# Raw weight rows of the second and third pair of w_up rows trade buffers, and the last write moves to another queue

## The chip, the cores and the metric

The kernel runs on one NeuronCore of a Trainium2 chip. What counts is the device time of one execution in microseconds (us), as the median of several runs. Beside it one execution was profiled: every engine's instructions and every transfer with its times. The engines are named as in the profile: PE (TensorE, with PEld for its weight loads), DVE (VectorE), ACT (ScalarE), POOL (GpSimd) and SP (SyncE, which here only issues transfers). An engine works through its own instructions in program order and waits on semaphores of others.

## The reference, cut to what matters

A decoder block for 1024 tokens of width 1024: a norm, two parallel branches (sparse attention and a state-space layer), a merge, and then an MLP and a final norm. The change touches only the MLP and the final norm:

```python
    x = x + merged @ w_out[l]
    h2 = rmsnorm(x, norm_mlp_g[l])
    x = x + jnp.square(jax.nn.relu(h2 @ w_up[l])) @ w_down[l]
return rmsnorm(x, norm_final_g)
```

`w_up` is 1024 x 4096 and `w_down` 4096 x 1024.

## The kernel before, in words

Every product is made of fp32 operands split in a high and a low part, with three matmuls each (high x high, low x high, high x low). A low part is raw minus high, so each weight tile costs a cast on ACT (the high part) and a subtraction on POOL or DVE (the low part) before PE can use it. The functions `cast` (L1091) and `weights` (L108) do that; a tile named `w` is such a pair.

The product with `w_up` is done as a two-by-two block scheme with seven products instead of eight. A *pair* q (0 to 15) is one step of it: two raw tiles of `w_up` (128 x 1024 fp32, 512 KB each), number 2q and 2q + 1. In the text, `raw0` is the first, and `a21` and `a22` are the halves of the second. From them come four weight tiles:

- `wo`, the cast of `raw0` as it was loaded (`open_high`/`open_low` for pairs 0 and 1, `prep_open` for the others);
- `wa`, the cast of the sum tile `sa`, which `prep_s` makes with two DVE operations (L1115, L1116); `prep_a` casts it, and then turns `raw0` into other sums in place with two more DVE operations (L1122, L1123);
- `wb`, the cast of that changed `raw0` (`prep_b`), and `wc`, the cast of `a22` (`prep_c`).

The PE side of a pair is `p1` and `p2` (with `wo`), `p6` and `p5` (with `wa`), `p7` and `p3` (with `wb`) and `p4` (with `wc`), 12 matmuls each. `p7`, `p6` and `p4` go on adding in one PSUM tile `pa` of the pair: `p4` may not touch it until the DVE addition of `p7` (L1161) has read it. `sums` then forms four tiles on DVE (L1182 to L1185) and writes the activations to DRAM.

The order is written out by hand: what stands earlier in the code stands earlier on its engine. Pair 0 is woven into the end of the norm, `norm_split` transposing normed rows on PE (L977), ACT casting them (L981) and DVE making their low parts (L986). Pairs 1 and 2 get their `wo`, `p1` and `p2` there too, early. `t3_chunk` and `t4_rows` build two more operands, T3 and T4, by the same three steps (T4 with two further DVE operations, L1058 and L1059). A loop over q from 1 to 15 follows, in which `up_raw(q + 2)` loads two pairs ahead, then the product with `w_down` (lines from L1401 on PE), which reads the activations back from DRAM, and last the final norm (`final_a`, `final_b`).

Raw tiles lie in one of two places: two buffers `raw` of the pool `wpool`, or one tile `raw2` (two raws in one) of `mpool`. Before, even pairs use the former and odd ones the latter. Pair 1 is the exception: its first raw is loaded early in a `raw` buffer (`r[1]`) and opened there, and later both raws are loaded again as `raw2`. Pair 2's first raw (`r2`, L1307) takes the buffer that `r[1]` leaves, and so its load waits for `open_low(1)` (L1109). The second (`r2b`, L1335) takes the buffer that pair 0's `raw0` leaves after `prep_b(0)`.

`ep` is a pool whose tag e4 has five buffers, for the normed rows `xs`, for the results `e1` and `e2` and for the gains.

Of the kernel before, what the change touches and what calls it, by code (L numbers as in the profile page):

```python
# [19 lines left out]
P = 128  # L20
S = 1024
# [44 lines left out]
def hybrid_block(ctx: ExitStack, tc: tile.TileContext, a: dict, out: bass.AP, dbg=None):  # L66
    nc = tc.nc
# [35 lines left out]
    def load(pool, src, n):  # L103
        raw = pool.tile([P, n], F32, name="raw", tag="raw", bufs=nbuf[0])
        nc.sync.dma_start(raw, src)
        return raw
# [64 lines left out]
    wpool = ctx.enter_context(tc.tile_pool(name="wpool", bufs=1))  # L171
# [3 lines left out]
    with ExitStack() as st1:  # L175
        pss = {}
        for c in PO1:
            nm, n = {"d": ("dps", DP1), "s": ("sps", SP1), "x": ("xps", XP1)}[c]
# [464 lines left out]
    with ExitStack() as st2:  # L643
        pss = {}
        for c in PO2:
            nm, n = {"s": ("ssp", SB), "t": ("tps", CB), "o": ("ops", OB)}[c]
# [23 lines left out]
        def prep(g, b):  # L670
            qT = ap_.tile([P, 6, P], F32R, name="qT", tag="qT", bufs=2)
            nc.sync.dma_start(f32(qT), q_d[g][b])

            for n in range(b + 1):
                if (g, n) in vT:
                    continue
                hf, o = n // 4, (n % 4) * P
                for j in range(2):
                    if (g, j, hf) not in kT:
                        kT[g, j, hf] = kp.tile([P, 2, 512], F32R, name="kT", tag="kT", bufs=6)  # L680
                    nc.sync.dma_start(f32(kT[g, j, hf][:, :, o:o + P]), k_d[g][n][:, j])
                vT[g, n] = kp.tile([P, 2, 2, 64], F32R, name="vt", tag="vt", bufs=9)
                nc.sync.dma_start(f32(vT[g, n]), v_d[g][n])
            return qT, gates[:, g, b]
# [148 lines left out]
        first, second = [], []  # L833
# [39 lines left out]
    with ExitStack() as st3:  # L873
# [6 lines left out]
        def e4(name, shape=(P, S)):  # L880
            return ep.tile(list(shape), F32, name=name, tag="e4")

        def s4(name, shape):
            return ep.tile(list(shape), F32, name=name, tag="s4", bufs=S4B)
# [76 lines left out]
        c1, c2 = slice(0, 512), slice(512, 1024)  # L961
# [26 lines left out]
        def split_to(name, b, pt):  # L988
            low(*high(name, b, pt))
# [33 lines left out]
        def norm_d3(b):  # L1023
            V.tensor_tensor(xr[b][:, c1], xs[b][:, c2], xs[b][:, c1], op=ALU.subtract)
# [66 lines left out]
        def cast(x, n):  # L1091

            w = wpool.tile([P, 2, S], F32R, name="w", tag="w", bufs=nbuf[1])
            A.copy(w[:, 0, :n], x)  # L1094
            G.tensor_tensor(w[:, 1, :n], x, f32(w[:, 0, :n]), op=ALU.subtract)  # L1095
            return w

        def prep_open(q, raw0):
            u = us[q] = Pair()
            u.wo = cast(raw0, S)  # L1100
# [10 lines left out]
        def prep_s(q):  # L1111

            u = us[q]
            u.sa = s4("sa", (P, S))
            V.tensor_tensor(u.sa[:, c2], u.a21, u.a22, op=ALU.add)  # L1115
            V.tensor_tensor(u.sa[:, c1], u.sa[:, c2], u.raw0[:, c1], op=ALU.subtract)  # L1116

        def prep_a(q):
            u = us[q]
            u.wa = cast(u.sa, S)  # L1120

            V.tensor_tensor(u.raw0[:, c1], u.raw0[:, c1], u.a21, op=ALU.subtract)  # L1122
            V.tensor_tensor(u.raw0[:, c2], u.raw0[:, c2], u.sa[:, c1], op=ALU.subtract)  # L1123

        def prep_b(q):
            us[q].wb = cast(us[q].raw0, S)
# [4 lines left out]
        def p1(q):  # L1131
            u = us[q]
            u.pa, u.e1 = acc("pa"), e4("e1", (P, 2, 512))
            prod(u.pa, u.wo[:, :, c1], "B11", True)
            A.copy(u.e1[:, 0], u.pa)

        def p2(q):
            u = us[q]
            pb = acc("pb")
            prod(pb, u.wo[:, :, c2], "B21", True)  # L1140
            V.tensor_tensor(u.e1[:, 0], u.e1[:, 0], pb, op=ALU.add)

        def p2_square(q):
            square(us[q].e1[:, 0])

        def p6(q):
            u = us[q]
            u.e2 = e4("e2", (P, 2, 512))
            prod(u.pa, u.wa[:, :, c1], "T2", False)
            A.copy(u.e2[:, 0], u.pa)  # L1150

        def p5(q):
            u = us[q]
            u.pc = acc("pc")
            prod(u.pc, u.wa[:, :, c2], "T1", True)
            A.copy(u.e2[:, 1], u.pc)

        def p7(q):
            u = us[q]
            prod(u.pa, u.wb[:, :, c1], "T3", False)  # L1160
            V.tensor_tensor(u.e2[:, 1], u.e2[:, 1], u.pa, op=ALU.add)  # L1161
            square(u.e2[:, 1])

        def p3(q):
            u = us[q]
            prod(u.pc, u.wb[:, :, c2], "B22", False)
            V.tensor_tensor(u.e2[:, 0], u.e2[:, 0], u.pc, op=ALU.add)
# [24 lines left out]

        def up_raw(q):

            if q % 2:
                t = mpool.tile([P, 2, S], F32, name="raw2", tag="m")
                for i in range(2):
                    nc.sync.dma_start(t[:, i], a["w_up"][2 * q + i])
                raws[q] = t[:, 0], t[:, 1]
            else:  # L1200
                raws[q] = [load(wpool, a["w_up"][2 * q + i], S) for i in range(2)]

        def set_raws(q, raw0, a21, a22):
            us[q].raw0, us[q].a21, us[q].a22 = raw0, a21, a22

        def half_raws(q):
            r0, r1 = raws[q]
            set_raws(q, r0, r1[:, c1], r1[:, c2])
# [8 lines left out]
        def load_acts(k):  # L1217
            if k < 56:
                raw = wpool.tile([P, 2, 512], F32, name="raw", tag="raw", bufs=nbuf[0])
                nc.sync.dma_start(raw, act_d[k % 8][:, LEFT[k // 8]])  # L1220
                araw.append(raw)

        def fetch(u):

            n, q = divmod(u, 16)
            if n == 0:
                if q % 2 == 0:
                    xy.append(oppool.tile([P, 2, 2, 512], F32, name="xy", tag="opT"))
                dst, i, j = xy[q // 2][:, q % 2, 0], 0, 0
            elif n == 1:  # L1230
                dst, i, j = xy[q // 2][:, q % 2, 1], 0, 1
            elif n in (2, 5):
                if q % 4 == 0:
                    z.append(mpool.tile([P, 4, 512], F32, name="z", tag="m"))
                dst, i, j = z[-1][:, q % 4], 1, int(n == 2)
            else:
                return
            nc.scalar.dma_start(dst, a["w_down"][2 * q + i][:, j * 512:j * 512 + 512])  # L1238
# [53 lines left out]
        r = [load(wpool, a["w_up"][2 * q], S) for q in range(2)]  # L1292
# [11 lines left out]
                norm_d3(b - 1)  # L1304
            norm_b(b, (lambda: open_low(1)) if b == 7 else None)
        norm_d3(7)
        r2 = load(wpool, a["w_up"][4], S)  # L1307
        p1(0)
        for f in norm_split(6):
            low(*f)  # L1310
# [21 lines left out]
        t4 = [t4_rows(4), t4_rows(5)]  # L1332
        split_to("T4", 4, t4[0])
        split_to("T4", 5, t4[1])
        r2b = load(wpool, a["w_up"][5], S)  # L1335
        p5(0)
        t4 += [t4_rows(6), t4_rows(7)]
        split_to("T4", 6, t4[2])
        split_to("T4", 7, t4[3])
        up_raw(1)  # L1340
        half_raws(1)
        p7(0)
        prep_s(1)
        prep_a(1)
        p3(0)
        prep_b(1)
        p3_square(0)
# [3 lines left out]
        for q in range(1, 16):  # L1351
            n = q + 1
            if q + 2 < 16 and q > 0:
                up_raw(q + 2)
            if q == 15:
                for k in range(2):
                    load_acts(k)
            if q >= 3:
                p1(q)
                p2(q)  # L1360
            if n < 16 and n > 2:
                prep_open(n, raws[n][0])
                half_raws(n)
            if n == 2:
                set_raws(2, r2, r2b[:, c1], r2b[:, c2])
            if q >= 3:
                p2_square(q)
            if n < 16:
                prep_s(n)
            p6(q)  # L1370
            p5(q)
            if n < 16:
                prep_a(n)
            else:
                for u in range(AHEAD):
                    fetch(u)
            p7(q)
            if n == 16:
                prep(0)
            p3(q)  # L1380
            if n < 16:
                prep_b(n)
            p3_square(q)
            if n == 16:
                prep(1)
            p4(q)
            if n < 16:
                prep_c(n)
            else:
                prep(2)  # L1390
            sums(q)


        y = []
# [30 lines left out]
            rstds[b] = ep.tile([P, 1], F32, name="rstd", tag="rstd")  # L1425
            G.tensor_tensor(rstds[b], sq[:, 0:1], neghalf, op=ALU.pow)

        def final_b(b):
            V.scalar_tensor_tensor(y[b][:, c1], y[b][:, c1], rstds[b], gfin[:, c1], op0=ALU.mult, op1=ALU.mult)  # L1429
            nc.sync.dma_start(out[b * P:(b + 1) * P, c1], y[b][:, c1])  # L1430
            A.activation(y[b][:, c2], y[b][:, c2], AF.Copy, scale=rstds[b])
            nc.sync.dma_start(out[b * P:(b + 1) * P, c2], y[b][:, c2])

        for n in range(7):
            ps, first, (r, cs) = groups[n % 2], n in (0, 1, 5), DST[n]
# [22 lines left out]
            for b in range(4):  # L1458
# [4 lines left out]
                else:  # L1463
# [3 lines left out]
                    final_a(4 + b)  # L1467
                    if b:
                        final_b(3 + b)
        final_b(7)  # L1470


def host_layout(inp):
# [71 lines left out]
```

## Time and profile before

| what | value |
|---|---|
| median of 3 runs | 1545.28 us (1545.13 to 1545.9) |
| the profiled execution, its own time | 1545.69 us |
| its span from first to last instruction | 1543.6 us |
| PE busy | 1513.3 us (98%) |
| DVE, ACT, POOL busy | 1048.8, 752.4, 443.5 us |

The profiled execution is 0.41 us over the median, and 2.1 us of its time lie outside the span. The stretch of the change lies between 905 and 950 us of the span; the last writes are issued from 1538 us on. Most rows below are timelines: start, duration, engine, line, operation, output <- inputs, shapes, count, and in brackets how long the engine had been idle and for whom. In a timeline neighbours of one kind are put together (x2, x12).

### The profile page before, as it was taken

The numbers are of one execution on the slowest core, as the hardware profiler recorded it, in microseconds if no ns is written. First come the engines' busy times: TensorE is split into PE (matmuls) and PEld (weight loads), VectorE is DVE, ScalarE is ACT, GpSimd is POOL, SyncE is SP. The second block draws the span as 40 slices with busy tenths as digits, with TensorE's granted clock in tenths as the row PEclk, the third lists the DMA queues.
The fourth block names the chain that finished last, engine by engine and source line by source line (L and its number), as shares of the span: only waits on it lengthen the run. The fifth ranks groups of instructions, "written<-read, shape, count | busy, mean of one in ns | idle before, by whom it ended". The sixth has DMA issues, their size and how long they took to land. (4 is left out here: it accounts for less than half of the span.)

```text
span 1543.6 us, 22375 instructions
## 1 busy us (share of the span) xinstructions
PE 1513.3 (98%) x7938; PEld 1273.8 (83%) x7938; DVE 1048.8 (68%) x1869; ACT 752.4 (49%) x1555; POOL 443.5 (29%) x428
## 2 busy tenths in 40 slices
PE   7999999999999999999999999999999999999997
PEld 6789999888888888888888877888888778888886
DVE  7995886358988978674552377655555467757676
ACT  6343535247766766542221455555555434444454
POOL 3113535221001101000000024444444354545454
PEclk9999999999999999999999999999999999999999
DMA  6435455652113211283335114544443587533633
GB/s 230 140 93 155 142 159 179 175 174 74 45 49 110 62 59 52 66 283 121 96 99 187 69 55 160 181 150 150 145 147 132 168 281 247 177 110 100 193 117 137
DMA packets 113504, 211.09 MB, mean 137 GB/s; under 512 B 14704, under 2 KB 49520, under 8 KB 113392
## 3 DMA queue, kind: packets, MB, share of 16 engines
q1 hardware_dynamic: 104176, 192.87, 38.1%
q10 hardware_dynamic: 9216, 16.78, 3.2%
q8 instruction: 63, 1.03, 0.3%
q14 instruction: 49, 0.40, 0.1%
HBM read 139.36 MB, written 68.16 MB: 134 GB/s over the span
## 5 line engine op out<-in xcount | busy, mean ns | idle before, releaser
L1401 PE MATMUL pg<-w 128*128 128x512 f32 x1344 | 307.6, 390 | 3.4 <-DVE w L1271 1.8
L1401 PEld LDWEIGHTS pg<-w 128*128 128x128 f32 x1344 | 252.2, 188 | 58.7 <-DVE w L1271 3.3
L150 PE MATMUL ps_m<-hT,w 128*128 128x512 f32 x768 | 215.2, 400 | 0.4 <-ACT mst L156 0.3
L1269 POOL TENSOR_TENSOR w<-raw,w 128x512 fp32r<-128x512 f32 x112 | 154.4, 1381 | 159.6 <-ACT w L1268 153.0
L150 PEld LDWEIGHTS ps_m<-hT,w 128*128 128x128 f32 x768 | 130.6, 188 | 21.5 <-ACT mst L156 0.8
L1268 ACT CAST w<-raw 128x512 fp32r<-128x512 f32 x112 | 69.4, 620 | 158.4 <-PE pg L1401 93.8
L1079 PE MATMUL pa<-T,w 128*128 128x512 f32 x576 | 141.7, 395 | 1.1 <-POOL w L1095 1.1
L1079 PEld LDWEIGHTS pa<-T,w 128*128 128x128 f32 x576 | 108.1, 188 | 26.7 <-POOL w L1095 1.6
L1095 POOL TENSOR_TENSOR w<-raw,w 128x1024 fp32r<-128x1024 f32 (+1 forms) x45 | 95.5, 2125 | 100.4 <-ACT w L1094 100.4
L1271 DVE TENSOR_TENSOR w<-xy,w 128x512 fp32r<-128x512 f32 x64 | 87.2, 1372 | 46.4 <-ACT w L1270 33.1
L112 POOL TENSOR_TENSOR w<-raw,w 128x1024 fp32r<-128x1024 f32 (+1 forms) x27 | 70.8, 2624 | 162.6 <-ACT w L111 162.6
L769 ACT ACTIVATE p<-s_ps,sst 128x640 f32<-128x640 f32 (+7 forms) x128 | 90.0, 707 | 23.5 <-PE pt L804 13.4
L1271 DVE TENSOR_TENSOR w<-z,w 128x512 fp32r<-128x512 f32 x48 | 62.5, 1304 | 38.3 <-ACT w L1270 36.8
L763 PE MATMUL s_ps<-kT,qT 128*128 128x512 f32 (+3 forms) x384 | 85.8, 337 | 0.2
L804 PE MATMUL pt<-ident,p 128*128 128x128 f32 x528 | 83.8, 275 | 2.1 <-DVE pl__5079 L708 1.0
L1002 POOL TENSOR_TENSOR rstd<-ss,neghalf 128x1 f32<-128x1 f32 x8 | 4.8, 599 | 280.8 <-DVE ss L1000 280.8
L766 DVE CUSTOM_DVE_ANT_0 s_ps<-s_ps,cmask 128x256 f32<-128x256 f32 (+7 forms) x96 | 63.9, 677 | 19.6 <-PE s_ps L763 19.1
L119 PE MATMUL ps_a<-w,hT 128*128 128x256 f32 (+1 forms) x256 | 75.7, 296 | 0.0
L118 PE MATMUL ps_a<-w,hT 128*128 128x256 f32 (+1 forms) x256 | 75.6, 295 | 0.0
L120 PE MATMUL ps_a<-w,hT 128*128 128x256 f32 (+1 forms) x256 | 75.0, 293 | 0.0
L763 PEld LDWEIGHTS s_ps<-kT,qT 128*128 128x128 f32 x384 | 63.7, 188 | 11.6 <-ACT p L769 1.4
L804 PEld LDWEIGHTS pt<-ident,p 128*128 128x128 f32 x528 | 62.4, 140 | 12.4 <-PE s_ps L763 1.3
(1438 smaller groups left out, 3505.5 us busy)
## 6 DMA issues: line engine op xcount, KB each, us to landing
raw<-act_d SPq DMA_DIRECT2D x56, 512.0 KB
raw<-w_up SPq DMA_DIRECT2D x32, 512.0 KB
act_d<-ts SPq DMA_DIRECT2D x16, 1024.0 KB
raw<-w_mg SPq DMA_DIRECT2D x16, 512.0 KB
mg_d<-mst SPq DMA_DIRECT2D x32, 256.0 KB
act_d<-e SPq DMA_DIRECT2D x16, 512.0 KB
xy<-w_down ACTq DMA_DIRECT2D x32, 256.0 KB
z<-w_down ACTq DMA_DIRECT2D x32, 256.0 KB
```

Of the source, the lines that this page charges most:

```text
L118: T.matmul(ps, lhsT=wh, rhs=xh, start=first and i == 0, stop=False)
L119: T.matmul(ps, lhsT=wl, rhs=xh, start=False, stop=False)
L120: T.matmul(ps, lhsT=wh, rhs=xl, start=False, stop=last and i == n - 1)
L150: m = T.matmul(ps, lhsT=w[:, e, ks], rhs=hT[k][:, r, hs], start=k == 0 and i == 0, stop=k == KD - 1 and i == 2)
L763: T.matmul(s_ps[:, o:o + hi - lo], lhsT=qT[:, 2 + hp * 2 + j, :], rhs=kT[g, br, hf][:, e, lo - hf * 512:hi - hf * 512], start=e == 0, stop ...
L769: A.activation(pp[j][:, 0:w], row, AF.Exp, scale=-1.0, bias=st[:, 0, j:j + 1], accum_out=st[:, 2, j:j + 1])
L804: T.transpose(pt[:, i, j, :], c[hp, br][j][:, (i0 + i) * P:(i0 + i + 1) * P], ident)
L1079: T.matmul(ps, lhsT=w[:, e, ks], rhs=x[:, k], start=first and k + i == 0, stop=k == 3 and i == 2, skip_group_check=not first)
L1095: G.tensor_tensor(w[:, 1, :n], x, f32(w[:, 0, :n]), op=ALU.subtract)
L1269: G.tensor_tensor(w[:, 0, 1], raw, f32(w[:, 0, 0]), op=ALU.subtract)
L1271: V.tensor_tensor(w[:, 1, 1], t, f32(w[:, 1, 0]), op=ALU.subtract)
L1401: T.matmul(ps, lhsT=w[:, 0, e, bs], rhs=w[:, 1, r], start=first and q + i == 0, stop=q == 15 and i == 2, skip_group_check=not first)
```

## The change

Pair 1 now keeps its opened raw (`r[1]`) as its `raw0` and loads only its second raw (`r1b`), in the buffer that pair 0 leaves. Pair 2's first raw is loaded early in an e4 buffer (`rawo`), opened from there, and later both its raws are loaded as `raw2` of `mpool`; from there on even pairs use `mpool` and odd ones `wpool`. `prep_s(1)` and `prep_a(1)` move ahead: the first to before `p5(0)`, the second to before `p7(0)`. The second write of the last row block is issued from ACT's queue instead of SP's. The number of loads and of computing instructions stays the same.

```diff
         def up_raw(q):
-            if q % 2:
+            if q % 2 == 0:
                 t = mpool.tile([P, 2, S], F32, name="raw2", tag="m")
...
         norm_d3(7)
-        r2 = load(wpool, a["w_up"][4], S)
+        r2 = e4("rawo")
+        nc.sync.dma_start(r2, a["w_up"][4])
         p1(0)
...
         split_to("T4", 5, t4[1])
-        r2b = load(wpool, a["w_up"][5], S)
+        r1b = load(wpool, a["w_up"][3], S)
+        set_raws(1, r[1], r1b[:, c1], r1b[:, c2])
+        prep_s(1)
         p5(0)
         t4 += [t4_rows(6), t4_rows(7)]
         split_to("T4", 6, t4[2])
         split_to("T4", 7, t4[3])
-        up_raw(1)
-        half_raws(1)
+        up_raw(2)
+        half_raws(2)
+        prep_a(1)
         p7(0)
-        prep_s(1)
-        prep_a(1)
         p3(0)
         prep_b(1)
...
-            if n == 2:
-                set_raws(2, r2, r2b[:, c1], r2b[:, c2])
...
-        def final_b(b):
+        def final_b(b, second=nc.sync):
...
-            nc.sync.dma_start(out[b * P:(b + 1) * P, c2], y[b][:, c2])
+            second.dma_start(out[b * P:(b + 1) * P, c2], y[b][:, c2])
...
-        final_b(7)
+        final_b(7, nc.scalar)
```

On DVE, from the low parts of T4's first two blocks to the addition of `p3(0)`, the order before is this (`pt` is a transposed block in PSUM, `tt` a work tile of T4, `e` the results of a pair, `sa` and `raw` tiles of pair 1):

```order
L1058 TENSOR_TENSOR tt<-B_9448,pt 128x512
L1059 TENSOR_TENSOR tt<-tt,B_9449 128x512
L1058 TENSOR_TENSOR tt<-B_9448,pt 128x512
L1059 TENSOR_TENSOR tt<-tt,B_9449 128x512
L986 TENSOR_TENSOR T_9968<-tt,T_9967 128x4x128 x2
L1161 TENSOR_TENSOR e_9953<-e_9953,pa 128x512
L1115 TENSOR_TENSOR sa<-raw_10023 128x512
L1116 TENSOR_TENSOR sa<-sa,raw_10023 128x512
L1122 TENSOR_TENSOR raw_10023<-raw_10023 128x512
L1123 TENSOR_TENSOR raw_10023<-raw_10023,sa 128x512
L1167 TENSOR_TENSOR e_9953<-e_9953,pc 128x512
```

and after the change, from the same place, it is this:

```order
L1115 TENSOR_TENSOR sa<-raw 128x512
L1116 TENSOR_TENSOR sa<-sa,raw 128x512
L1058 TENSOR_TENSOR tt<-B_9448,pt 128x512
L1059 TENSOR_TENSOR tt<-tt,B_9449 128x512
L1058 TENSOR_TENSOR tt<-B_9448,pt 128x512
L1059 TENSOR_TENSOR tt<-tt,B_9449 128x512
L986 TENSOR_TENSOR T_9968<-tt,T_9967 128x4x128 x2
L1122 TENSOR_TENSOR raw<-raw 128x512
L1123 TENSOR_TENSOR raw<-raw,sa 128x512
L1161 TENSOR_TENSOR e_9953<-e_9953,pa 128x512
L1167 TENSOR_TENSOR e_9953<-e_9953,pc 128x512
```

All four operations of pair 1's `prep_s` and `prep_a` now stand ahead of the addition of `p7(0)`, L1161; before, they stood behind it.

On ACT the difference at the same place is the cast of `sa` (the high part of `wa` of pair 1; L1083 and L1084 are the two steps of a square):

```order
 L981 CAST T_9967<-tt 128x4x128 x2
+L1094 CAST w<-sa 128x1024
 L1083 ACTIVATE e_9953<-e_9953 128x512
 L1084 ACTIVATE e_9953<-e_9953 128x512
-L1094 CAST w<-sa 128x1024
-L1094 CAST w<-raw_10023 128x1024
+L1094 CAST w<-raw 128x1024
 L1083 ACTIVATE e_9953<-e_9953 128x512
 L1084 ACTIVATE e_9953<-e_9953 128x512
```

It moved from behind the squares of `p7(0)` to right behind the casts of T4's last two blocks.

SP's queue, from the last write of `x_d` (the normed stage's rows) to the first activations:

```order
 L995 DMA x_d_160<-x_9117 128x1024
-L105 DMA raw<-w_up 128x1024 x2
-L1198 DMA raw_10023<-w_up 128x1024 x2
+L1308 DMA rawo<-w_up 128x1024
+L105 DMA raw<-w_up 128x1024
+L1198 DMA raw_10026<-w_up 128x1024 x2
 L1187 DMA act_d_161<-e_9772 128x2x512
```

The count and the places of the loads are the same; the first of them now fills an e4 buffer, which was last read in the transposes of row block 4.

## Rows read from the trace of the kernel before

**Rows 1.** The page, part 1: busy time and share of the span.

```profile
PE 1513.3 (98%) x7938; PEld 1273.8 (83%) x7938; DVE 1048.8 (68%) x1869; ACT 752.4 (49%) x1555; POOL 443.5 (29%) x428
```

**Rows 2.** Busy time by stretch: PE, PEld, DVE, ACT, POOL; PEclk; DMA share; GB/s.

```profile
946.00:1224.00 278.00, 278.00 (x1200) 225.19 (x1199) 161.81 (x160) 143.03 (x212) 123.25 (x57) 1.00 0.45 158
928.40:938.70 10.30, 10.30 (x54) 8.57 (x53) 9.73 (x16) 4.57 (x8) 1.28 (x1) 1.00 0.32 120
```

**Rows 3.** Timeline of PE, 921 to 947 us.

```profile
925.44 1.25 PE L977 MATMUL pt<-ident,x 128*128 128x128 f32 x8 [1.15 <-DVE T L986]
...
939.43 3.12 PE L1079 MATMUL pa<-T,w 128*128 128x512 f32 x13
943.68 2.79 PE L1079 MATMUL pa<-T,w 128*128 128x512 f32 x11 [1.13 <-POOL w L1095]
```

**Rows 4.** Timeline of SP's queue, 904.6 to 931 us.

```profile
904.63 0.32 SPq L995 DMA_DIRECT2D x_d<-x  x1
908.44 18.05 SPq L105 DMA_DIRECT2D raw<-w_up  x2
```

**Rows 5.** Timeline of ACT, 909 to 945 us.

```profile
909.19 0.61 ACT L981 CAST B<-pt 128x512 fp32r<-128x512 f32 x1
911.89 1.05 ACT L1094 CAST w<-raw 128x1024 fp32r<-128x1024 f32 x1 [2.10 <-DMA raw<-w_up]
914.00 0.63 ACT L1083 ACTIVATE e<-e 128x512 f32<-128x512 f32 x1 [1.05 <-DVE e L1141]
...
936.75 0.63 ACT L981 CAST T<-tt 128x512 fp32r<-128x512 f32 x1 [0.70 <-DVE tt L1059]
```

**Rows 6.** Timeline of POOL: at 913 us, and at 1492 to 1497 us.

```profile
913.02 2.42 POOL L1095 TENSOR_TENSOR w<-raw,w 128x1024 fp32r<-128x1024 f32 x1 [6.34 <-ACT w L1094]
...
1492.18 1.78 POOL L1269 TENSOR_TENSOR w<-raw,w 128x512 fp32r<-128x512 f32 x1 [1.18 <-ACT w L1268]
1494.96 1.30 POOL L1269 TENSOR_TENSOR w<-raw,w 128x512 fp32r<-128x512 f32 x1 [1.00 <-ACT w L1268]
```

**Rows 7.** Timeline of DVE, 1491 to 1497 us.

```profile
1492.13 0.68 DVE L1257 TENSOR_TENSOR z<-z,xy 128x512 f32<-128x512 f32 x1
1492.74 1.77 DVE L1271 TENSOR_TENSOR w<-z,w 128x512 fp32r<-128x512 f32 x1
```

**Rows 8.** Timeline of DVE, 908 to 926 us.

```profile
910.88 0.69 DVE L1024 TENSOR_TENSOR x<-xs 128x512 f32<-128x512 f32 x1
...
924.70 1.29 DVE L986 TENSOR_TENSOR T<-pt,T 128x512 fp32r<-128x512 f32 x2 [3.27 <-ACT T L981]
```

**Rows 9.** Timeline of DVE, 936 to 942 us.

```profile
936.63 1.47 DVE L986 TENSOR_TENSOR T<-tt,T 128x512 fp32r<-128x512 f32 x2
938.01 0.68 DVE L1161 TENSOR_TENSOR e<-e,pa 128x512 f32<-128x512 f32 x1
...
941.27 0.68 DVE L1167 TENSOR_TENSOR e<-e,pc 128x512 f32<-128x512 f32 x1
```

**Rows 10.** Timeline of PE, at two of its waits.

```profile
193.40 0.33 PE L432 MATMUL pk<-ident,k 128*128 128x128 f32 x1 [1.81 <-DVE k L429]
...
1235.90 0.50 PE L1401 MATMUL pg<-w 128*128 128x512 f32 x1 [1.76 <-DVE w L1271]
```

**Rows 11.** Busy time by stretch, around rows 10's waits; columns as in rows 2.

```profile
189.00:191.00 2.00, 2.00 (x19) 2.00 (x19) 1.38 (x4) 1.58 (x5) 1.92 (x5) 1.00 0.18 66
199.20:201.20 2.00, 2.00 (x11) 2.00 (x11) 1.97 (x6) 1.15 (x3) 0.01 (x1) 0.50 0.51 144
194.70:201.40 6.70, 5.77 (x28) 5.47 (x27) 6.63 (x11) 1.32 (x4) 4.51 (x11) 0.50 0.29 91
1236.00:1246.00 10.00, 8.76 (x36) 6.58 (x36) 3.21 (x3) 2.30 (x5) 2.59 (x3) 1.00 0.90 343
```

**Rows 12.** Timeline of SP's queue, 1540 to 1544 us: the last write.

```profile
1540.14 0.41 SPq L1432 DMA_DIRECT2D out_dram<-y  x1
```

**Rows 13.** Busy time of the stretch with the last writes; columns as in rows 2.

```profile
1539.30:1542.20 2.90, 0.00 (x0) 0.00 (x0) 0.39 (x1) 0.36 (x1) 0.00 (x0) 0.54 0.96 362
```

## The prediction

> **What bounds the kernel now.** The page comes first: PE is busy 98% of the span, every other engine 68% or less [rows 1]. A table of busy time by stretch says where that holds: from 946 to 1224 us, pairs 1 to 15, PE is busy all 278.00 us at granted clock 1.00, or 0.232 us per matmul [rows 2]. A late transfer or a busier DVE in there costs nothing before PE itself waits, so the change is worth what it does to PE's waits before 946 and to the end after the last matmul. PE's timeline shows two waits near the edit: 1.15 us before the transposes at 925.44, for DVE's low part L986, and 1.13 us before `p6(1)` at 943.68, for POOL's low part of `wa` [rows 3]. Removing both could give 2.3 us at most. The second table row shows what stands beside them: from 928.40 to 938.70 DVE is busy 9.73 of 10.30 us, so there it is nearly as full as PE [rows 2].
>
> **The first load, earlier.** Before, the load for pair 2 waited on SP for `open_low(1)` and was issued at 908.44; ACT's cast of it began at 911.89 after 2.10 us of idling, that is 3.45 us after the issue [rows 4, 5]. Afterwards it fills an e4 buffer and can follow the last `x_d` write, 904.63 + 0.32 = 904.95 [rows 4]; by the same 3.45 us the data can be used at about 908.4, or 909.2 if it lands more slowly behind that write. So the cast starts behind ACT's own cast of 909.19 (0.61 us), at about 909.75, ends at 910.80 (1.05 us), and POOL's low part of `wo` starts 0.08 us later as it did before (911.89 + 1.05 to 913.02) [rows 5, 6]: about 910.85. The earlier cast by itself gains nothing: ACT's next instruction, at 914.00, waited 1.05 us for DVE's L1141 in any case [rows 5].
>
> It puts POOL in DVE's way, however. At 1492 us DVE began L1257 first, at 1492.13, and POOL's subtraction, begun 0.05 us later, took 1.78 us where the same shape takes 1.30; the DVE instruction behind it, begun at 1492.74, took 1.77 instead of 0.68 and ended at 1494.51, 0.55 us after POOL's end at 1493.96 [rows 6, 7]. So one holds the other off for an entire instruction, and a waiting POOL goes ahead of DVE's next. DVE's L1024, which like those reads two operands in SBUF (both halves of `xs`), starts at 910.88 [rows 8]; POOL comes 0.03 us before it. If POOL wins, it runs 2.42 us [rows 6], L1024 ends at 910.88 + 2.42 + 0.55 = 913.85 instead of 911.57, and what is queued behind it on DVE (the low parts L986, then L1141 for which ACT waits at 914.00) is 2.2 us late. The slack does not absorb that: ACT waits for DVE at 914.00, and DVE for ACT 3.27 us at 924.70 [rows 5, 8], so this is one chain of hand-overs that ends at PE's wait at 925.44 [rows 3]. Cost 2.2; 0 if DVE wins.
>
> **`prep_s(1)` and `prep_a(1)` ahead of `p7(0)`.** The same four DVE operations now stand in front of L1161, where DVE is full. From L1161's start at 938.01 to the next addition at 941.27 five operations take 3.26 us, 0.65 each [rows 9]; four are 2.6. Queued behind them is L1161, and `p4(0)`, which began on PE at 939.43, waits for it. L1161 ends at 938.69 + 2.6 = 941.3, `p4(0)` starts near 941.4, and its 13 matmuls end at 941.4 + 13 x 0.232 = 944.4, where `p6(1)` began at 943.68 [rows 3]. `wa` is ready by then, so the wait of 1.13 is gone and yet the net is +0.7.
>
> A second meeting of POOL and DVE comes on top. L1115 and L1116, 1.3 us, stand ahead of T4's last low parts, so ACT's T4 cast moves from 936.75 to 938.05 (to 938.68); the cast of `wa` follows it, to 939.73, and POOL starts at 939.8 [rows 5]. On DVE, L1122 starts at 938.01 + 1.3 = 939.3 and L1123, with two operands in SBUF, at 939.95 [rows 9]. POOL is first by 0.15: L1123 is held until 939.8 + 2.42 = 942.2 and ends at 942.8, L1161 at 943.4, `p4(0)` starts at 943.5 and ends at 946.5, 2.8 after 943.68. I take 2.8; the bounds are 0.7 (DVE first) and, with every wait hidden, -1.1.
>
> **PE's clock after longer waits.** The trace has one fall of the granted clock far from both ends: PE idled 1.81 us up to 193.40 [rows 10], and from 194.70 to 201.40 the clock was 0.50, that is 1.2 of 2.4 GHz [rows 11]. An idle time of 1.76 up to 1235.90 did not bring one: the clock is 1.00 in the ten microseconds behind it [rows 10, 11]. In full work PE did 11 matmuls in 2 us there against 19 in 2 us before it [rows 11], a loss of 42%. The stretch was 6.7 us long, with PE idle for 0.93 of it; for a single wait I choose two thirds of that, 4.6 us. The second meeting makes PE idle from 939.43 to 943.5, over 4 us, well over 1.81; the fall came 3.1 us after that idle time began (194.7 - 191.6), so here near 942.6, and the low clock ends near 947.2: (947.2 - 943.5) x 0.42 = 1.6. The first makes the idle time of 1.15 at most 3.3, part of it spread over earlier transposes; a fall there costs up to 4.6 x 0.42 = 1.9, of which I take 1.0, since the chain there is ACT's and DVE's as much as PE's. Bounds of the two: 0 and 1.9 each.
>
> **The other loads.** Pair 1's second raw and the pair of `raw2` loads are issued where two loads and two loads were; the row of 908.44 spans 18.05 us up to the second of them, issued near 926.2 [rows 4]. With the 3.45 us from issue to use that is 929.7. `prep_s(1)` needs it only when DVE is through with T4's fourth and fifth blocks, 2.6 us (four operations) ahead of 936.63, near 934 [rows 9]: four us later. Cost 0, or what a landing after 934 is late. From 946 on the buffers of even and odd pairs have merely traded names, and PE hides them as before [rows 2].
>
> **The last write.** It was issued at 1540.14, behind another on SP [rows 12]. From 1539.30 to 1542.20 the transfer engines are 96% busy at 362 GB/s [rows 13], so an earlier issue meets transfers still under way. I take 0.1 of gain; bounds 0 and 0.41, the duration of that issue [rows 12]. By the Trainium skill ("Trainium Kernel Development and Optimization", section "Key Constraints") transfers from SP's, ACT's and POOL's queues run on the same 16 engines, and issuing from several saves only the issue time; by that rule alone the gain would be the full issue of 0.41 and the sum 0.3 lower. The row of 96% leaves no place for most of that.
>
> **Sum.** 2.2 + 1.0 (first meeting and its clock) + 2.8 + 1.6 (second) - 0.1 = +7.5. The profiled execution took 1545.69 us (2.1 outside the span), so 1553.2; it stands 0.41 over the median of 1545.28, so 1552.8.
>
> **The rivals.**
> - Only the second meeting costs: the early load lands 0.1 us later than worked out, and L1024 goes first. 2.8 + 1.6 - 0.1 = +4.3, 1549.6; 1548.0 without the clock. For it: the margin of 0.03 is below what I can work out of a landing. Against it: the shorter landing leaves 0.8 us in hand, and then the cast waits for ACT alone.
> - Only the first costs: DVE is first at L1123, the margin there being 0.15. 2.2 + 1.0 + 0.7 - 0.1 = +3.8, 1549.1.
> - Neither costs: +0.7 - 0.1, 1545.9, within 0.2% (3.1 us, about what a measurement of this kernel can tell from no change). With a clock fall after the 2 us of idle time, 1547.5.
> - Faster: DVE has more room than the 0.57 us that the stretch shows, because its operations start sooner when `pt` is there sooner, and L1161 ends before 939.4 despite the four. Then the waits of 1.13 and the 0.41 go: 1543.7. It decides at 939.4; the saturated stretch speaks against it.
>
> **How the numbers follow.** Both meetings .42, only the second .24, only the first .13, neither .16, faster .05. Both: 1550.2 (no clock loss) to 1555.3 (1.9 each, and 0.7 more for a later landing of `wa`). The range 1546.5 to 1555.5 leaves out the faster case, half of the neither case, and a little above. Faster by over 0.2% needs 1542.2, below the faster case itself: .03. Same takes the neither case and the low edges of the single ones, .20; slower .77.
>
> **What would show it.** In the new trace: the `rawo` load issued near 905; POOL's `wo` at 910.85 with L1024 stretched from 0.69 to near 3; the transposes of 925.44 near 927.7. L1123 stretched to near 2.9; PE idle over 3 us before `p4(0)`; no wait before `p6(1)`; a clock of 0.50 for some us after 942. From then to the end a constant shift, PE without waits as in [rows 2]. I am wrong if L1024 and L1123 keep 0.69, if PE's clock stays at 1.00, or if a new wait appears behind 950 with the traded buffers.

## The result and the profile after

The changed kernel takes 1554.8 us (median of 6 runs, 1551.5 to 1555.46) beside 1545.53 us (6 runs, 1544.19 to 1545.94) for the kernel before: 1.0056 times the time, 95% interval 1.0047 to 1.0066. It is slower by 0.56%, or 9.3 us, where +7.5 was forecast. The profiled execution took 1554.82 us, with a span of 1553.0 us against 1543.6.

The page, part 1, answers to [rows 1]: PE did the same 7938 instructions and was busy 1.6 us longer. DVE's sum grew by 4.9 us, and two instructions shown below, both held up, make 4.35 of that (2.90 - 0.69 and 2.83 - 0.69); ACT's and POOL's sums are the same. So what was lost is mostly waiting.

```profile
PE 1514.9 (98%) x7938; PEld 1274.2 (82%) x7938; DVE 1053.7 (68%) x1869; ACT 752.4 (48%) x1555; POOL 443.2 (29%) x428
```

PE's timeline, with idle time and its releaser in the brackets, answers to [rows 3]; the row at 904.62 is the last wait ahead of the change, and its row in the kernel before stands under it.

```profile
904.62 2.82 PE L1079 MATMUL pa<-B,w 128*128 128x512 f32 x11 [1.00 <-DVE w L1109]
...
928.20 1.25 PE L977 MATMUL pt<-ident,x 128*128 128x128 f32 x8 [2.34 <-DVE T L986]
...
946.26 7.32 PE L1079 MATMUL pa<-T,w 128*128 128x512 f32 x24 [3.93 <-DVE e L1161]
```

```profile
904.06 2.82 PE L1079 MATMUL pa<-B,w 128*128 128x512 f32 x11 [1.00 <-DVE w L1109]
```

Against before, the three rows stand 0.56, 2.76 and 6.83 us later (904.62 - 904.06, 928.20 - 925.44, 946.26 - 939.43). The 0.56 arises ahead of the first changed instruction. So the first place costs 2.20 and the second 4.07; at the second, `p4(0)` and `p6(1)` now run as one row of 24 matmuls, and the wait of 1.13 before `p6(1)` is gone.

DVE's timeline around both places answers to [rows 8, 9], POOL's to [rows 6], ACT's and SP's to [rows 5] and [rows 4]. Two rows show the first meeting, 911.37 on POOL and 911.44 on DVE:

```profile
911.44 2.90 DVE L1024 TENSOR_TENSOR x<-xs 128x512 f32<-128x512 f32 x1
...
927.46 1.29 DVE L986 TENSOR_TENSOR T<-pt,T 128x512 fp32r<-128x512 f32 x2 [3.27 <-ACT T L981]
...
942.08 0.68 DVE L1122 TENSOR_TENSOR raw<-raw 128x512 f32<-128x512 f32 x1
942.68 2.83 DVE L1123 TENSOR_TENSOR raw<-raw,sa 128x512 f32<-128x512 f32 x1
945.43 0.68 DVE L1161 TENSOR_TENSOR e<-e,pa 128x512 f32<-128x512 f32 x1
```

```profile
911.37 2.41 POOL L1095 TENSOR_TENSOR w<-rawo,w 128x1024 fp32r<-128x1024 f32 x1 [4.14 <-ACT w L1094]
...
942.52 2.44 POOL L1095 TENSOR_TENSOR w<-sa,w 128x1024 fp32r<-128x1024 f32 x1 [9.01 <-ACT w L1094]
```

```profile
909.74 0.61 ACT L981 CAST B<-pt 128x512 fp32r<-128x512 f32 x1
910.22 1.08 ACT L1094 CAST w<-rawo 128x1024 fp32r<-128x1024 f32 x1
```

```profile
905.19 0.32 SPq L995 DMA_DIRECT2D x_d<-x  x1
905.61 0.37 SPq L1308 DMA_DIRECT2D rawo<-w_up  x1
```

L1024 took 2.90 instead of 0.69 ([rows 8]) and L1123 2.83 instead of 0.69, its row in the kernel before:

```profile
940.66 0.69 DVE L1123 TENSOR_TENSOR raw<-raw,sa 128x512 f32<-128x512 f32 x1
```

Each ends a little over half a microsecond behind POOL's instruction (914.34 and 913.78; 945.51 and 944.96). Busy time by stretch (PE, PEld, DVE, ACT, POOL; granted clock; DMA share; GB/s) shows the rest:

```profile
928.00:946.00 18.00, 14.13 (x72) 11.38 (x72) 15.59 (x22) 7.29 (x12) 4.62 (x3) 1.00 0.24 88
...
947.70:951.00 3.30, 3.30 (x9) 2.58 (x8) 1.40 (x1) 2.31 (x4) 2.41 (x1) 0.50 0.00 0
951.10:954.40 3.30, 3.30 (x16) 2.69 (x15) 3.27 (x5) 1.75 (x4) 1.52 (x1) 1.00 0.51 195
956.00:1235.00 279.00, 279.00 (x1204) 225.87 (x1202) 160.41 (x155) 145.52 (x217) 122.50 (x57) 1.00 0.44 155
1254.90:1258.20 3.30, 3.30 (x10) 2.56 (x9) 3.30 (x3) 0.75 (x2) 3.30 (x3) 0.50 0.82 261
```

The clock stayed at full speed after the 2.34 us wait. It went to half (1.2 of 2.4 GHz) after the one of 3.93, for 9 matmuls in 3.30 us where 16 ran afterwards. It did so once more at 1254.9, where nothing was changed. Between 956 and 1235 us PE is busy all the time, as in [rows 2]. PE's two waits in the product with `w_down`, and the last two issues of the run, answer to [rows 10] and [rows 12]:

```profile
1243.00 8.09 PE L1401 MATMUL pg<-w 128*128 128x512 f32 x34 [1.76 <-DVE w L1271]
1252.59 0.50 PE L1401 MATMUL pg<-w 128*128 128x512 f32 x1 [1.50 <-ACT w L1270]
```

```profile
1549.04 0.33 SPq L1430 DMA_DIRECT2D out_dram<-y  x1
```

```profile
1549.01 0.38 ACTq L1432 DMA_DIRECT2D out_dram<-y  x1
```

In the kernel before, the second of these waits and SP's issue of the same line (L1430) were:

```profile
1244.89 0.49 PE L1401 MATMUL pg<-w 128*128 128x512 f32 x1 [0.90 <-ACT w L1270]
```

```profile
1539.72 0.33 SPq L1430 DMA_DIRECT2D out_dram<-y  x1
```

The account of the profiled execution: 0.56 before the change; 2.20 at the first place; 4.07 - 1.13 = 2.94 at the second; then the row of 1235.90 stands 7.10 later (1243.00), which leaves 7.10 - 0.56 - 2.20 - 2.94 = 1.40, put down to the low clock. The wait after it, 0.90 before (at 1244.89) and 1.50 now (at 1252.59), adds 0.60, and the rest up to SP's last issue (1539.72 to 1549.04, 9.32), in which the second stretch of low clock lies, 1.62. Together 9.32; the span grew by 9.4.

### The profile page after: what moved, and what is told of

It is laid out like the page before. It is cut to its first block, busy times and chain, and to the rows that moved or that the text cites. A ratio compares the mean times of both kernels' runs of the same rounds, so it can differ in the third digit from the quotient of the medians.

```text
span 1553.0 us, 22378 instructions
## 1 busy us (share of the span) xinstructions
PE 1514.9 (98%) x7938; PEld 1274.2 (82%) x7938; DVE 1053.7 (68%) x1869; ACT 752.4 (48%) x1555; POOL 443.2 (29%) x428
```

## The experiments

The theory is the prediction's: at two places POOL's subtraction holds a DVE instruction that PE's next work hangs on. At the second, four more DVE operations stand ahead of L1161, and PE's clock falls with its wait there. The rivals: the traded buffers, the early load or the last write cost the time; or DVE's queue alone does, without POOL. Kernels of one group ran on one chip; each group is compared with its own runs of the kernel before.

**x1: the kernel before with the last write alone.**

```diff
-        final_b(7)
+        final_b(7, nc.scalar)
```

> The kernel before with only the last write moved to ACT's queue. The theory of the prediction: the transfer engines are full there, so -0.1 us (bounds 0 and -0.41), about 1545.2, no other difference. The rival, that the trailing write is what made part of the change slow (an issue from ACT that delays the last row block), gives +0.3 us or more. A low granted clock near 1245 us of the span in this kernel too would say that the second fall of the clock in the changed kernel (from 1254.9 to 1258.1 us) is not the change's own.

Measured: 1545.63 beside 1545.6 us, 0.9999 (0.9990 to 1.0008). Its two last issues:

```profile
1538.88 0.38 ACTq L1432 DMA_DIRECT2D out_dram<-y  x1
```

```profile
1538.91 0.33 SPq L1430 DMA_DIRECT2D out_dram<-y  x1
```

The last write goes out next to the other one, and the span ends 3.89 us after the latter (1542.8). Before, it ended 3.88 us after it (1543.6 - 1539.72), though the last issue came 0.42 later. So the edit shows neither cost nor gain; the interval of the medians, some 1.4 us to either side, is too wide for a gain of 0.1 to 0.4, and only the trace speaks to that. No low clock shows near 1245 us here.

**x2: `prep_s(1)` and `prep_a(1)` back behind `p7(0)`.**

```diff
-        prep_s(1)
         p5(0)
...
-        prep_a(1)
         p7(0)
+        prep_s(1)
+        prep_a(1)
         p3(0)
```

> The changed kernel with prep_s(1) and prep_a(1) put back behind p7(0); buffers, early load and last write stay changed. Theory (two meetings of POOL and DVE): L1123 and L1161 are no longer late, p4(0) follows p3(0) without a wait, the wait of 1.13 us before p6(1) is back, no clock fall near 947 us. L1024 stays stretched to 2.9 us, so +2.2 us of the first meeting remain: 1547.6; with the second clock fall of about 2 us near 1254 us, if that comes from the traded buffers, 1549.6. Rival (the traded buffers or the loads cost the time): it stays near 1554.8.

Measured: 1549.12 beside 1545.6, 1.0023 (1.0013 to 1.0033). PE's timeline, and the clock behind its first wait:

```profile
927.13 1.28 PE L977 MATMUL pt<-ident,x 128*128 128x128 f32 x8 [2.40 <-DVE T L986]
...
946.92 2.81 PE L1079 MATMUL pa<-T,w 128*128 128x512 f32 x11 [1.20 <-POOL w L1095]
```

```profile
928.30:931.60 3.30, 3.30 (x9) 2.58 (x9) 1.29 (x2) 2.74 (x5) 0.45 (x1) 0.50 0.49 159
946.92:1239.00 292.08, 290.41 (x1249) 234.69 (x1249) 174.56 (x167) 152.27 (x230) 131.40 (x63) 1.00 0.46 158
```

The second place is as before, its wait of 1.13 back as 1.20; the first remains. What was not expected: here the clock fell after the first place's wait, and PE did 9 matmuls in 3.30 us.

**x3: `norm_d3(7)`, DVE's L1024 at the first place, moved behind the addition of `p2(0)`.** The load, the cast and POOL's work stay.

```diff
-        norm_d3(7)
         r2 = e4("rawo")
...
         p2(0)
+        norm_d3(7)
         p2_square(0)
```

> The changed kernel with norm_d3(7), which is DVE's L1024 there, moved behind the addition of p2(0), 2.4 us later, out of POOL's way; the early load and its cast stay. Theory: POOL's low part of wo (2.41 us) meets no DVE instruction with two SBUF operands, L1141 is on time, the transposes near 928.2 start about 2.2 us earlier; L1024 takes 0.69 again. The second meeting stays. 1552.6; without the second clock fall near 1254 us 1550.6. Rival (the first 2.2 us come from the early load or cast themselves, not from L1024 being held): 1554.8, with DVE's chain as late as before.

Measured: 1549.99 beside 1545.6, 1.0032 (1.0019 to 1.0044). The profiled execution was its slowest (1552.87). POOL's subtraction, DVE's row of L1024, PE's two waits, and the clock around the second:

```profile
910.96 2.42 POOL L1095 TENSOR_TENSOR w<-rawo,w 128x1024 fp32r<-128x1024 f32 x1 [4.14 <-ACT w L1094]
```

```profile
913.41 0.68 DVE L1024 TENSOR_TENSOR x<-xs 128x512 f32<-128x512 f32 x1
```

```profile
924.96 1.25 PE L977 MATMUL pt<-ident,x 128*128 128x128 f32 x8 [0.53 <-DVE T L986]
...
943.02 8.61 PE L1079 MATMUL pa<-T,w 128*128 128x512 f32 x24 [3.92 <-DVE e L1161]
```

```profile
942.40:949.10 6.70, 6.08 (x14) 4.79 (x15) 3.77 (x5) 3.95 (x6) 2.39 (x1) 0.50 0.01 2
```

POOL's subtraction ran at 910.96 for 2.42 us and met no such DVE instruction. L1024 took 0.68, and PE's wait fell from 2.34 to 0.53, below the 1.15 of the kernel before. So neither load nor cast is what cost there. The second wait stayed.

**x4: L1122 and L1123 behind L1161; L1115, L1116 and the cast of `sa` stay early.** Lines behind the edit count four or five higher: L1165 is L1161, L1126 is L1122.

```diff
             u.wa = cast(u.sa, S)
+            if q != 1:
+                prep_a2(q)
+        def prep_a2(q):
+            u = us[q]
...
         prep_a(1)
         p7(0)
+        prep_a2(1)
```

> The changed kernel with pair 1's L1122 and L1123 moved behind p7(0)'s addition L1161; L1115, L1116 and the cast of sa stay early. Theory: L1161 is late by two DVE operations (1.3 us) alone, p4(0) waits about 0.6 us instead of 3.93, p6(1) waits for nothing as wa is early; L1123 is still held by POOL, but only L1167 and wb stand behind it. No clock fall near 947. Of the +9.3 us 2.2 of the first meeting stay, less 0.6: 1547.1; 1549.1 with a clock fall near 1254 us. Rival (DVE's queue alone delays L1161, no hold by POOL): the gain against the changed kernel would be 1.3 us only, 1553.5.

Measured: 1548.04 beside 1545.6, 1.0018 (1.0009 to 1.0027). DVE and PE at the second place:

```profile
940.24 0.68 DVE L1165 TENSOR_TENSOR e<-e,pa 128x512 f32<-128x512 f32 x1
940.84 2.78 DVE L1126 TENSOR_TENSOR raw<-raw 128x512 f32<-128x512 f32 x1
```

```profile
941.07 5.71 PE L1079 MATMUL pa<-T,w 128*128 128x512 f32 x24 [0.58 <-DVE e L1165]
```

POOL still holds a DVE instruction (L1122 now), but nothing that PE waits for stands behind it: the wait is 0.58 instead of 3.93. Had DVE's queue alone made the wait, taking two operations of about 0.65 out of it would have given back 1.3.

**x6: the low part of pair 1's `wa` made by DVE behind L1161**, the order ahead of it as changed.

```diff
-            u.wa = cast(u.sa, S)
+            if q == 1:
+                u.wa = wpool.tile([P, 2, S], F32R, name="w", tag="w", bufs=nbuf[1])
+                A.copy(u.wa[:, 0], u.sa)
+            else:
+                u.wa = cast(u.sa, S)
...
         p7(0)
+        V.tensor_tensor(us[1].wa[:, 1], us[1].sa, f32(us[1].wa[:, 0]), op=ALU.subtract)
```

> The changed kernel with the low part of pair 1's wa made by DVE behind L1161 instead of by POOL: the order ahead of L1161 stays (four operations early), only POOL's part in the second meeting is taken away. Theory: L1123 takes 0.69, L1161 is late by the four operations alone (2.6 us), p4(0) waits 2.0 instead of 3.93; p6(1) may wait some tenths for the low part on DVE. 1.9 us less idle time and, if the clock keeps 1.00, 1.4 us less again than the changed kernel: 1551.4 beside 1554.8. Rival (the place in DVE's queue makes all of the loss): 1554.8, p4(0) waiting 3.9 as before.

Measured: 1550.82 beside 1544.98, 1.0035 (1.0022 to 1.0049), with the widest spread of all (1545.84 to 1553.78). L1123 is L1127 here:

```profile
942.93 0.68 DVE L1127 TENSOR_TENSOR raw<-raw,sa 128x512 f32<-128x512 f32 x1
```

```profile
944.36 6.85 PE L1079 MATMUL pa<-T,w 128*128 128x512 f32 x22 [1.86 <-DVE e L1165]
```

That splits the wait of 3.93: 1.86 from the four operations, and the remaining 2.07 from POOL. The clock did not keep 1.00, though: it was 0.50 from 944.8 to 948.1 after this wait of 1.86 too, and once more after each of the waits of 2.33 and 1.78 at 926.86 and 1241.09.

**x0: the changed kernel once more.**

> The changed kernel once more, unaltered. Theory: both meetings are set by the order of the instructions and so are there again: L1024 and L1123 near 2.9 us each, PE's waits of 2.34 before the transposes near 928 and of 3.9 before p4(0), granted clock 0.50 for 3 to 7 us after that. Open: whether the clock falls again near 1254 us. If it does with a load landing 9.0 us or more after ACT's last cast there, that fall belongs to the order of pair 1's sums by a way not yet seen; if the landing is near 8.3 us without a fall, it is the spread of a transfer.

Measured: 1552.57 beside 1544.98, 1.0053 (1.0041 to 1.0065). The profiled execution was its slowest (1556.08). Its PE waits, and the stretches of low clock:

```profile
929.45 1.71 PE L977 MATMUL pt<-ident,x 128*128 128x128 f32 x8 [2.38 <-DVE T L986]
...
949.03 2.47 PE L1079 MATMUL pa<-T,w 128*128 128x512 f32 x5 [4.00 <-DVE e L1161]
```

```profile
930.00:933.30 3.30, 3.30 (x11) 2.78 (x11) 1.47 (x3) 2.65 (x5) 0.13 (x1) 0.50 0.47 159
947.10:953.80 6.70, 4.77 (x11) 3.81 (x12) 3.81 (x4) 3.36 (x5) 3.04 (x2) 0.50 0.01 2
1247.40:1250.70 3.30, 3.30 (x9) 2.54 (x9) 1.25 (x2) 0.00 (x0) 0.09 (x1) 0.50 1.02 395
```

Both meetings are there again, with the same sizes (L1024 and L1123 took 2.90 and 2.83). The low clock is not the same: it came after the 2.38 us wait this time, lasted twice as long at the second place, where it began inside the wait (at 947.1, the wait ended at 949.03), and in the product with `w_down` it followed the wait before 1246.41, not the later one.

**x7: 24 transposes of the identity on PE between `p3(0)` and `p4(0)`**, added work that nobody reads.

```diff
         p3_square(0)
+        for _ in range(6):
+            pt = dps.tile([P, 4, P], F32, name="pt", tag="p", bufs=2)
+            for k in range(4):
+                T.transpose(pt[:, k, :], ident, ident)
         p4(0)
```

> The changed kernel with 24 transposes of the identity into PSUM tiles that nobody reads, on PE between p3(0) and p4(0): added work that fills 3.1 to 3.4 of the 3.93 us in which PE waits, and delays nothing. Theory: the granted clock stays 1.00 after 946 us, p4(0) and p6(1) run at full speed, 1.4 us less than the changed kernel: 1553.4 beside 1554.8. Rival (the low clock there is not for the waiting): clock 0.50 again and no gain.

Measured: 1550.53 beside 1544.98, 1.0036 (1.0024 to 1.0048), 2.0 us under x0 on the same chip. PE's timeline and the clock behind it:

```profile
942.06 2.78 PE L1353 MATMUL pt<-ident 128*128 128x128 f32 x24
946.21 5.05 PE L1079 MATMUL pa<-T,w 128*128 128x512 f32 x21 [1.37 <-DVE e L1161]
```

```profile
946.30:949.60 3.30, 3.30 (x15) 2.71 (x16) 0.40 (x2) 3.24 (x6) 1.19 (x1) 1.00 0.00 0
```

More work on PE went with a shorter time: `p4(0)` starts as late as before, but at full clock, with 15 matmuls in 3.30 us instead of 9. One profile of a thing that comes and goes is weak evidence by itself; the median of 2.0 us less, with the intervals of x0 and x7 overlapping a little, goes the same way. That the filling kept the clock up is thus likely, not shown.

**x5 and x9: both mends of x3 and x4**, in two groups of runs.

> Both mends together: norm_d3(7) behind the addition of p2(0), and pair 1's L1122 and L1123 behind p7(0)'s addition. Theory: neither L1024 nor L1161 is late by POOL; the transposes near 925 wait 0.5 instead of 1.15 (-0.6 us), p4(0) waits about 0.6, p6(1) loses its 1.13 (-0.5): 1.1 us under the kernel before, 1544.5 beside 1545.6, within what the measurement can tell; 1546.5 with a clock fall near 1250 us. Rival (traded buffers, early load or last write cost by themselves): 2 us or more above the kernel before at 1240 us of the span already.

> Both mends once more, for the comparison on one chip. Theory: PE's waits in 900 to 950 us sum to 2.1 us (1.0, 0.5, 0.6) against 3.3 before; 1544.9, the same as the kernel before within what the measurement can tell; a clock of 0.50 for 3.4 us near 1236 to 1256 us in some executions only. Rival (the traded buffers cost by themselves): 1546.5 or more.

Measured: 1544.96 beside 1544.98, 0.9997 (0.9988 to 1.0006), and 1543.93 beside 1545.7, 0.9992 (0.9983 to 1.0001). PE's waits in x5:

```profile
925.07 1.25 PE L977 MATMUL pt<-ident,x 128*128 128x128 f32 x8 [0.53 <-DVE T L986]
...
939.76 5.73 PE L1079 MATMUL pa<-T,w 128*128 128x512 f32 x24 [0.57 <-DVE e L1165]
```

All of the loss is gone, to within some 1.4 us, with the traded buffers, the early load and the moved write in place. PE's waits at the two places sum to 1.1 us against 2.3 before.

**x8: both mends, and transposes of the identity into PE's waits in the product with `w_down`.**

```diff
+                for k in range({3: 12, 6: 6}.get(q, 0) if n == 0 else 0):
+                    T.transpose(groups[1][0][:, k % 4 * P:k % 4 * P + P], ident, ident)
                 for b in range(4):
                     mms(ps[b], first, q, held[16 * n + q], b)
```

> Both mends, and in the product with w_down 12 transposes of the identity ahead of the matmuls with the fourth weight tile and 6 ahead of the seventh, into a PSUM tile that starts anew later: they fill some 1.4 of the 1.76 us and 0.7 of the 0.9 to 1.9 us in which PE waits there in every kernel of this study. Theory (a wait of PE brings the fall of the clock): no granted clock of 0.50 between 1230 and 1262 us, in which x5_both lost some 1 us; 1544.0 beside 1545.0 for the kernel before, a difference that the measurement can hardly tell. Rival (the falls there come from the transfers or the load at that time): the clock falls as often, the transposes cost their own 2 us: 1546.

Measured: 1544.58 beside 1545.7, 0.9991 (0.9982 to 1.0000). The clock was 1.00 from 1236 to 1262 us in its profile, but in x9's too, without the transposes, and the medians of the two are 0.65 us apart the other way. Whether the filling helps there stays open. No version is shown to beat the kernel before: x8 and x9 are some 0.1% under it, at the edge of their intervals.

## Why the prediction was right

- **The early load gains nothing by itself.** As said. The cast waited for ACT's own work alone (909.74 + 0.61 to 910.22, no idle time), and ACT's next instruction waited 5.46 us for DVE instead of 1.05.
- **First meeting, +2.2.** Measured 2.20 (2.76 - 0.56), and in x0 2.20 again, if what those traces are late before 905 us is taken off (929.45 - 925.44, less 905.87 - 904.06). POOL was first by 0.07 us, forecast 0.03. Its chance looks put too low: in all six kernels with this order (the changed one, x0, x2, x4, x6, x7) POOL came 0.06 to 0.07 us ahead. A landing 0.1 us later, which the rival "only the second meeting" rested on, would not have decided it, since the cast waited for ACT. By the Trainium skill ("SBUF — State Buffer", section "🔬 SBUF: two separate sides") a POOL operation that reads SBUF and a DVE operation with two SBUF inputs share a pair of ports that whichever starts first keeps for the whole instruction; the trace agrees, with 2.90 and 2.83 us where 0.69 is the plain time. The rows also show an order: POOL's subtraction of 942.52 began inside L1122 (942.08, 0.68 us) and went ahead of L1123, as the prediction had read it from 1492 us.
- **Second place, +2.8 for the wait.** 2.94. `p4(0)` was forecast for 943.5, which with the 2.76 that was already lost is 946.26, the row's own time. x6 divides it as the prediction did: 1.86 of waiting for four operations (forecast 2.0), 2.07 for POOL.
- **Clock at the second place, +1.6.** 1.40 in the profile, but not by the course that was forecast. The clock was to fall inside the wait, 3.1 us after its start; it fell at about 947.6, 5.3 us after it (942.33) and after `p4(0)` had begun, and stayed low for 3.4 us instead of 4.6. So the nearness of 1.40 to 1.6 is partly luck. In x0 and x3 the fall did come inside the wait, the stretch was 6.7 us long, and by the same sum it cost 2.0 and 2.7.
- **Clock at the first place, +1.0.** Nothing in the profile, and about 1.5 where it fell (x2's trace stands 0.51 earlier at 903.55 and 3.25 later at 1239.15; of these 3.76 the meeting made 2.20). Six profiles have this wait of 2.33 to 2.40 us; the clock fell after it in three (x0, x2, x6). Taking about half of a fall's cost was a fair choice, but the reason given for it, that the chain there is ACT's and DVE's, was not what decided.
- **"From then to the end a constant shift".** This is the step that failed. The profile lost 2.2 more in the product with `w_down`: 0.60 by a load that landed later, 1.62 by a low clock behind that wait. The prediction had read that a wait of 1.76 there brings no fall; in x0, x5 and x6 the clock fell right behind this first wait (1.76 to 1.78). Whether the 2.2 are the change's is not shown. In every kernel but x8, where transposes fill it, PE waits there 1.70 to 1.78 us for DVE and then, in most, again for the load, and the clock fell after one of the two in the changed kernel, x0, x3, x4, x5 and x6, and not in the kernel before, x1, x2, x7 and x9. x2 has the same traded buffers and no fall. It was seen only with `prep_s(1)` early (six of eight profiles, without x8; none of three with it late). It also goes with the load: ACT's cast of it waited 8.52 to 9.53 us in the six that fell and 7.24 to 8.39 in the five that did not. But in x0, x5 and x6 the clock fell before that load was there, so a late landing can't be the cause in those. The same cast waited 9.04 us in x8, with PE's first wait filled, and no fall came. What decides stays open.
- **The last write, -0.1.** No gain in x1's trace; its median can't tell 0.1 from 0. By the Trainium skill ("Trainium Kernel Development and Optimization", section "Key Constraints") another queue saves the issue time alone; the trace agrees that the issue is 0.4 us sooner, and shows that the end, behind transfer engines that were 96% busy in the kernel before ([rows 13]), is not.
- **Traded buffers and the other loads, 0.** x5 and x9, which keep them, are level with the kernel before, and L1115, the first to need pair 1's second raw, began at 936.72 without a wait.

So +7.5 was the sum of terms of which two met their size within 0.15 (2.2 and 2.8). The clock's 2.6 at two places came out as 1.4 in one, and 2.2 came from a place not on the list, with 0.56 from the start of the trace. The mechanism of the two meetings is confirmed; that the total came as near as it did is in part luck: the two clock terms were too dear by 1.2 together, and the 2.2 was missing. The other group of runs, x0 with +7.6 us, is nearer to the sum than the first with +9.3. One sum of the prediction does not come out: its upper figure for both meetings, 1555.3, is 1554.7 by its own terms (1545.28 + 2.2 + 1.9 + 2.8 + 1.9 + 0.7 - 0.1). The measured 1554.8 lies just above that, with the 2.2 from behind 1235 us in it.

## What to carry to other kernels

Before work is pulled forward, set the start times of POOL's subtractions beside those of DVE's instructions with two SBUF operands: a few hundredths of a microsecond decide whether an instruction of 0.69 takes 2.9, and it matters only if PE's next work stands behind it. Moving one instruction (x3) and two (x4) out of the way gave all of it back when both were done (x5, x9); the load that looked late had never been what PE waited for. And a wait of PE like these (1.5 to 4.0 us) is counted with a possible surcharge for the clock, 1.4 to 2.7 us in these profiles, which one profile alone may not show.

## What the runs showed of the hardware that was not expected

The fall of the granted clock is not a property of the kernel but of the execution: after waits of 1.5 to 2.4 us it came in some profiles of the same order of instructions and not in others (the changed kernel and x0: no and yes after 2.34 and 2.38), during or after waits of 3.9 to 4.0 in all three (the changed kernel, x0, x3), and not in the one where 2.78 of 4.15 us were filled (x7). It is the same far ahead of anything that was changed, at the fall that the prediction took its figures from. There PE waits twice in every profile, up to about 193 and 198 us, and the clock went to 0.50 in eight of the twelve profiles and not in x1, x2, x6 and x8. Only in the kernel before did it fall ahead of the second wait, for 6.8 us; in the other seven it fell behind that one, for 3.4 us. So a length of 6.7 us and a delay of 3.1, as the prediction took them from one profile, were one draw of several. The kernel before has it too, by its other runs, though they do not show where: its 25 times in the first group of experiments lie between 1543.62 and 1548.6 us, with mean granted clocks of 0.999 in the fastest five and 0.995 to 0.997 in the slowest six.
